# Running sums seeded into PSUM and copied back by ScalarE, and the conditioning as sums of products along the free axis on VectorE

## The chip, the cores and the metric

The kernel runs on one core of a Trainium2 chip. The metric is device time of one execution in microseconds (us). Engines are named as in the profile: PE is TensorE (matrix products; PEld its weight loads), DVE is VectorE, ACT is ScalarE, POOL is GpSimd, SP is SyncE, whose in-order queue issues nearly all DMAs of this kernel. Every engine works through its own queue in order and waits there for the others by semaphores.

## The reference

One layer of a decoder block on 256 tokens of width 4096, in float32:

```
mod = silu(c) @ w_ada + b_ada                      # c: one row of 4096; w_ada 4096 x 12288
shift, scale, gate = split(mod, 3)
h = rmsnorm(x, norm_g) * (1 + scale) + shift       # 256 x 4096
a_b, a_c, a_x, a_z, b_v, b_g, b_z = split(h @ w_in)  # w_in 4096 x 14336, seven parts of 2048
y_a = a_b * conv3(a_c * a_x) * silu(a_z)           # causal, depthwise
y_b = silu(layernorm(conv31(b_v * sigmoid(b_g)))) * silu(b_z)
x = x + gate * (concat(y_a, y_b) @ w_out)          # w_out 4096 x 4096
out = rmsnorm(x, final_g)
```

## The kernel before

**Products.** Each operand of the two projections is split in two 12-bit parts, and three of the four cross products are summed: hi*hi, hi*lo, lo*hi. A *step* loads 512 KB of weights (2 contraction tiles of 128 by 512 columns) into a tile of the pool `raws`; ScalarE writes the high part (`w_h`, L143), VectorE the low part (`w_l`, L144, raw minus high), and TensorE makes 12 products of 128x128 by 128x512 (2 contraction tiles, 2 token tiles, 3 products, L156 to L158). The pool `split` holds three steps' parts. There are 448 steps of the input projection and 128 of the output projection.

**Order of the products.** The 28 column tiles of the input projection are not finished one after the other: the 32 contraction tiles are cut into six blocks (`BLOCKS`), and in each block every column tile gets its products with that block's contraction tiles. A column tile in one block is a *segment* (`SEGS`). Its products build up in a PSUM tile `ps` (pool `pmm`, three buffers). After the first block ScalarE copies `ps` to SBUF as `acc` (L467); after each later block VectorE adds `ps` to `acc` (L469, 135 times in all). So the conditioning of a block's contraction tiles can be worked out while the products of earlier blocks run.

**Conditioning.** `silu(c) @ w_ada` is a product of one row with 201 MB of weights, loaded as 384 tiles of 512 KB: 256 for shift and scale (`mod`), 128 for the gate. For shift and scale, VectorE multiplies a tile by `silu(c)`, one value a partition, and adds it to `modacc` (L174); then TensorE sums over the partitions with one-column products with ones (`modps`, L197). Of the gate's four groups of 1024 columns, two are made on TensorE (`gateps`, L231, one-column weights, four side by side), two on VectorE (L174); each is summed over the partitions and spread to all of them by a product with a matrix of ones (`gatesum`, L248) and copied out by ScalarE (L240, L249).

**Background work.** `queue` holds closures with the step at which each is due; `next_w` first loads and splits the weights one step ahead (`AHEAD`), then runs what is due. The conditioning of contraction tile k is spread so that it is done before its first use; the gate is spread over four stretches of the last block and the output projection (`GATE_RUN`); the convolution of mixer B (30 taps for each of four groups: four ScalarE multiplications L370, one VectorE addition L371) runs from the last block into the output projection; the epilogue of mixer A and the layernorm of mixer B have their stretches too. Emitted in that order, the work of each engine stands in its queue in about that order.

**Start.** SyncE loads x.T and the conditioning of the first two contraction tiles; row statistics of x come from squares on ScalarE, additions on VectorE and products with ones on TensorE (L290). Then the first h (`make_h`) and the first products.

Of the kernel before, what the change touches and what calls it, by code (L numbers as in the profile page):

```python
# [37 lines left out]
GATE_PE = (0, 1)    # gate columns (1024 each) worked out on TensorE, the others on VectorE  # L38
GATE_RUN = {0: (0, 70), 1: (70, 115), 2: (115, 185), 3: (185, 231)}  # when, in steps from the last block on
# [16 lines left out]
PK = O_LNB + NB  # L56
# [23 lines left out]
UNITS = [[0, KD]]   # contraction tiles conditioned together: the first, their number  # L80
for _k in range(KD, KT, KD):
    if UNITS[1:] and UNITS[-1][1] == KD and FIRST_USE[_k] - FIRST_USE[_k - KD] < 4:
        UNITS[-1][1] += KD
    else:
        UNITS.append([_k, KD])


# [545 lines left out]
```

## Time and profile before

| | |
|---|---|
| time, three runs | 1729.15, 1729.73, 1729.89 us; median 1729.73 |
| profiled execution: span | 1728.9 us, 0.8 below that median |
| PE / DVE / ACT busy | 97% / 87% / 54% of the span |
| products of a step | 2.72 us with nothing between them |
| DMA | 522 MB, 302 GB/s on average |

The span is the time from the first to the last instruction of one profiled execution. Busy is the time in which an engine has at least one instruction at work. An instruction's shown duration overlaps its successor's on DVE, ACT and PE, so what it costs in a full queue is the distance from its start to the next start. PEld counts the weight loads of TensorE; line L156 has four in each step, so its count divided by four is a count of steps. In the names, `ps`, `pa` and `pb` are the PSUM tiles of the input projection and of the two halves of the output projection.

### The profile page before, as it was taken

Reading aid. Unit: us, or ns where it says so; the run is one execution under the profiler, and the core shown is the slowest. Engines: PE = TensorE matmul, PEld = TensorE weight load, DVE = VectorE, ACT = ScalarE, POOL = GpSimd, SP = SyncE. Lnnn points to the kernel's source line nnn. Section 1 sums busy time; section 2 is a strip of 40 time slices with the busy share of each in tenths; the row PEclk is TensorE's granted clock in tenths of the full one; section 3 lists DMA queues with packets and bytes.
Section 4 is the critical chain, followed back from the end, with each engine's and each line's share of the span. In section 5 each row is a group of like instructions: output and inputs, shape, how many; then the busy total and the mean of one; then the engine's idle time right before and its main releaser. Section 6 shows DMA issues by size and latency. Waiting matters only on the chain.

```text
span 1728.9 us, 21319 instructions
## 1 busy us (share of the span) xinstructions
PE 1669.5 (97%) x7480; PEld 1340.1 (78%) x7480; DVE 1506.9 (87%) x1490; ACT 937.0 (54%) x1304; POOL 2.9 (0%) x10
## 2 busy tenths in 40 slices
PE   2899999999999999999999999999999999999997
PEld 1778788888888888888888877777777887878885
DVE  7887998899898988898898857898998999989996
ACT  3555443443334333343333468888887888564443
POOL 0000000000000000000000000000000000000000
PEclk8899999999999999999999999999999999999998
DMA  9899899999999998999899977766888888779993
GB/s 387 327 317 331 300 344 327 325 320 332 310 335 326 330 326 302 312 352 329 292 340 321 327 243 248 253 230 232 288 278 281 277 286 280 266 254 335 361 345 116
DMA packets 145715, 522.42 MB, mean 302 GB/s; under 512 B 16196, under 2 KB 16196, under 8 KB 145608
## 3 DMA queue, kind: packets, MB, share of 16 engines
q1 hardware_dynamic: 145464, 520.71, 85.8%
q8 instruction: 58, 0.95, 0.2%
q10 hardware_dynamic: 144, 0.35, 0.1%
q14 instruction: 49, 0.40, 0.1%
HBM read 516.81 MB, written 4.19 MB: 301 GB/s over the span
## 4 chain that ended last, share of the span: by engine, by line
PE 86%; DVE 6%; DMA 4%; issue 3%; ACT 1%; SPq 0%; DVEq 0%; ACTq 0%
PE ps L156 23%; PE ps L157 23%; PE ps L158 23%; PE pb L158 3%; PE pb L156 3%; PE pb L157 3%; DVE w_l L144 2%; PE gateps L231 2%; DMA gate<-in_w_gate 2%; DVE cv L371 1%; PE pa L157 1%; PE pa L158 1%; DVE modacc L174 1%; PE pa L156 1%; DMA mod<-in_w_mod 1%
## 5 line engine op out<-in xcount | busy, mean ns | idle before, releaser
L143 ACT CAST w_h<-w_r 128x1024 fp32r<-128x1024 f32 x576 | 603.7, 1052 | 654.2 <-PE ps L158 490.4
L144 DVE TENSOR_TENSOR w_l<-w_r,w_h 128x1024 fp32r<-128x1024 f32 x576 | 700.8, 1220 | 118.8 <-ACT w_h L143 113.2
L156 PE MATMUL ps<-w_h,hT 128*128 128x512 f32 x1792 | 705.8, 394 | 3.0 <-ACT hT L162 2.6
L157 PE MATMUL ps<-w_l,hT 128*128 128x512 f32 x1792 | 700.7, 391 | 5.6 <-DVE w_l L144 5.6
L158 PE MATMUL ps<-w_h,hT 128*128 128x512 f32 x1792 | 699.4, 390 | 0.0
L156 PEld LDWEIGHTS ps<-w_h,hT 128*128 128x128 f32 x1792 | 337.5, 188 | 96.8 <-issue 10.8
L157 PEld LDWEIGHTS ps<-w_l,hT 128*128 128x128 f32 x1792 | 337.5, 188 | 79.9 <-DVE w_l L144 10.9
L158 PEld LDWEIGHTS ps<-w_h,hT 128*128 128x128 f32 x1792 | 337.3, 188 | 70.6
L174 DVE SCALAR_TENSOR_TENSOR modacc<-mod,cact,modacc 128x512 f32<-128x512 f32 (+1 forms) x341 | 337.4, 990 | 4.6 <-DMA mod<-in_w_mod 1.5
L370 ACT ACTIVATE pr<-uT,pks 128x255 f32<-128x255 f32 (+14 forms) x480 | 198.1, 487 | 2.1 <-DVE cv L371 1.6
L469 DVE TENSOR_TENSOR acc<-ps,acc 128x1024 f32<-128x1024 f32 x135 | 164.9, 1221 | 22.9 <-PE ps L158 22.4
L371 DVE TENSOR_TENSOR cv<-cv,pr 128x1020 f32<-128x1020 f32 (+14 forms) x120 | 138.7, 1156 | 27.1 <-ACT pr L370 26.4
L157 PE MATMUL pa<-w_l,yT 128*128 128x512 f32 x256 | 100.6, 393 | 2.4 <-DVE w_l L144 2.4
L156 PE MATMUL pa<-w_h,yT 128*128 128x512 f32 x256 | 100.1, 391 | 0.0
L156 PE MATMUL pb<-w_h,yT 128*128 128x512 f32 x256 | 100.1, 391 | 0.0
L158 PE MATMUL pb<-w_h,yT 128*128 128x512 f32 x256 | 100.0, 391 | 0.0
L158 PE MATMUL pa<-w_h,yT 128*128 128x512 f32 x256 | 100.0, 390 | 0.0
L157 PE MATMUL pb<-w_l,yT 128*128 128x512 f32 x256 | 99.6, 389 | 0.0
L174 DVE SCALAR_TENSOR_TENSOR gateacc<-gate,cact,gateacc 128x1024 f32<-128x1024 f32 x62 | 79.4, 1280 | 5.8 <-DMA gate<-in_w_gate 5.6
L157 PEld LDWEIGHTS pa<-w_l,yT 128*128 128x128 f32 x256 | 48.0, 188 | 14.6 <-DVE w_l L144 4.8
L467 ACT COPY acc<-ps 128x1024 f32<-128x1024 f32 x28 | 28.5, 1017 | 51.7 <-PE ps L158 51.7
L156 PEld LDWEIGHTS pb<-w_h,yT 128*128 128x128 f32 x256 | 48.1, 188 | 10.3 <-ACT w_h L143 0.2
(129 smaller groups left out, 645.2 us busy)
## 6 DMA issues: line engine op xcount, KB each, us to landing
w_r<-in_w_in SPq DMA_DIRECT2D x448, 512.0 KB, 5.2
mod<-in_w_mod SPq DMA_DIRECT2D x256, 512.0 KB, 5.1
gate<-in_w_gate SPq DMA_DIRECT2D x128, 512.0 KB, 4.8
w_r<-in_w_out SPq DMA_DIRECT2D x128, 512.0 KB, 5.1
xs<-in_xt SPq DMA_DIRECT2D x8, 512.0 KB, 10.2
xr<-in_x SPq DMA_DIRECT2D x8, 512.0 KB, 7.0
out<-o SPq DMA_DIRECT2D x16, 256.0 KB, 2.7
xc<-in_xt SPq DMA_DIRECT2D x4, 512.0 KB, 5.2
```

What stands on the lines that cost most here:

```text
L143: nc.scalar.copy(hi, raw)
L144: nc.vector.tensor_tensor(out=lo, in0=raw, in1=hi.bitcast(F32), op=ALU.subtract)
L156: nc.tensor.matmul(out, ah, hi[:, i], start=f, stop=False)
L157: nc.tensor.matmul(out, ah, lo[:, i], start=False, stop=False)
L158: nc.tensor.matmul(out, al, hi[:, i], start=False, stop=l)
L174: nc.vector.scalar_tensor_tensor(out=acc, in0=raw, scalar=cact[:, j:j + 1], in1=acc, op0=ALU.mult, op1=ALU.add)
L231: nc.tensor.matmul(state["ps"][r:r + 1, 0], cact[:, j + i:j + i + 1], raws_[i][:, h * CT:(h + 1) * CT], start=j == 0, stop=j == KT - 2)
L370: nc.scalar.activation(out=pr[:, j, sh:], in_=u[:, j, :S - sh], func=AF.Copy, scale=cbw[:, 4 * i + j, TAPS - 1 - sh:TAPS - sh])
L371: nc.vector.tensor_tensor(out=o[:, :, sh:], in0=o[:, :, sh:], in1=pr[:, :, sh:], op=ALU.add)
L467: nc.scalar.copy(acc[e], ps)
L469: nc.vector.tensor_tensor(out=acc[e], in0=ps, in1=acc[e], op=ALU.add)
```

## The change

Two things are rewritten, with what follows from them.

1. *Running sums.* `acc` is no longer added on VectorE. Before a segment with earlier sums, ScalarE copies `acc` into the PSUM tile (`seed`), the products add to it, and ScalarE copies the tile back (`take`, with Silu for the z tiles of mixer B). `take` is emitted in the next segment's first step, the seed of the next segment in the last step of the present one.
2. *Conditioning.* The weights are laid out transposed: the 128 outputs of a tile are the partitions, 1024 of the 4096 inputs lie along the free axis. `silu(c)` is spread once to all partitions (`cB`: four row loads, products with ones, Silu). A tile takes one VectorE instruction that multiplies it with its part of `cB` and sums along the free axis, started from the bias or the sum before; four of them make 128 outputs. No sum over partitions is left. The gate's 128 tiles are all done like this, spread over steps 0 to 170 from the last block on; the finished gate is transposed, written to device memory and loaded back spread over the partitions, in four loads beside those of `final_g`.
3. `raws` has 7 tiles instead of 10 (the room goes to `cB`); the row statistics of x are emitted ahead of the conditioning of the first two contraction tiles and summed over all of x on VectorE before TensorE; the first weights are loaded before the last four conditioning tiles. The comments are gone, so that line numbers differ.

```diff
-    raws = ctx.enter_context(tc.tile_pool(name="raws", bufs=10))
+    raws = ctx.enter_context(tc.tile_pool(name="raws", bufs=7))
...
+    def broadcast_c():
+        for q in range(D // ROW):
+            row = bigt(f"crow{q}", (P, ROW))
+            nc.sync.dma_start(row[:1], c[:, q * ROW:(q + 1) * ROW])
+            ps = pmm.tile([P, NS, CT], F32, tag="ps", name=f"cps{q}")
+            for h in range(2):
+                nc.tensor.matmul(ps[:, h], ones[:1], row[:1, h * CT:(h + 1) * CT], start=True, stop=True)
+            nc.scalar.activation(out=cB[:, q * ROW:(q + 1) * ROW], in_=ps, func=AF.Silu)
+
+    def ada_steps(name, srcs, bias, dst):
...
+        def step(q):
+            raw = rawt(f"{name}_{q}", (P, ROW))
+            nc.sync.dma_start(raw, srcs[q])
...
+            nc.vector.tensor_tensor_reduce(out=raw, in0=raw, in1=cB[:, q * ROW:(q + 1) * ROW], scale=1.0, scalar=p[:, q - 1:q] if q else bias, op0=ALU.mult, op1=ALU.add, accum_out=dst if q == D // ROW - 1 else p[:, q:q + 1])
...
+    def gate_finish():
+        ps = misc("gate_ps", (P, P))
+        nc.tensor.transpose(ps[:KT], gateT, ident)
+        row = rawt("gate_row", (P, P))
+        nc.scalar.copy(row[:KT], ps[:KT])
+        nc.sync.dma_start(gate_d.rearrange("(k p) -> k p", p=P), row[:KT])
...
-    for ci, (t0, t1) in GATE_RUN.items():
-        spread(gate_steps(ci), start_last + t0, start_last + t1)
+    spread(gate_steps(), start_last + GATE_RUN[0], start_last + GATE_RUN[1])
...
+    def seed(n):
+        _, e, k0, _ = SEGS[n]
         ps = pmm.tile([P, NS, CT], F32, tag="ps", name=f"ps{k0}_{e}")
-        for k in range(k0, k1, KD):
-            parts = next_w()
-            step += 1
-            products(ps, hT, parts, k, k == k0, k + KD == k1)
-        if k0 == 0:
+        if k0:
+            nc.scalar.copy(ps, acc[e])
+        return ps
+
+    def take(e, k1, ps):
+        if e not in acc:
             acc[e] = bigt(f"acc{e}")
-            nc.scalar.copy(acc[e], ps)
-        else:
-            nc.vector.tensor_tensor(out=acc[e], in0=ps, in1=acc[e], op=ALU.add)
+        nc.scalar.activation(out=acc[e], in_=ps, func=AF.Silu if k1 == KT and e >= 24 else AF.Copy)
...
+    ps = seed(0)
+    for n, (b, e, k0, k1) in enumerate(SEGS):
+        for k in range(k0, k1, KD):
+            parts = next_w()
+            step += 1
+            while pending:
+                pending.pop()()
+            if k + KD == k1 and n + 1 < len(SEGS):
+                ps_next = seed(n + 1)
+            products(ps, hT, parts, k, k == 0, k + KD == k1, seeded=k0 > 0)
+        pending.append(lambda e=e, k1=k1, ps=ps: take(e, k1, ps))
+        ps = ps_next
```

How the queues change is shown at three places. The first is VectorE's queue in the last block, from the split of step 401's weights on, before (`cv` with `pr`: a convolution tap; `yfA`: the epilogue of mixer A):

```order
L144 TENSOR_TENSOR w401_l_9319<-w401_r_9316,w401_h_9318 128x1024
L371 TENSOR_TENSOR cv1_7999<-cv1_7999,pr1_16_9322 128x4x240
L469 TENSOR_TENSOR acc13_606<-ps24_13_9209,acc13_606 128x1024
L144 TENSOR_TENSOR w402_l_9346<-w402_r_9343,w402_h_9345 128x1024
L371 TENSOR_TENSOR cv1_7999<-cv1_7999,pr1_17_9349 128x4x239
L326 TENSOR_TENSOR acc1_653<-acc1_653,acc13_606 128x1024
L144 TENSOR_TENSOR w403_l_9380<-w403_r_9377,w403_h_9379 128x1024
L340 SCALAR_TENSOR_TENSOR yfA1_0_9355<-psA4_9356,pks_88,yfA1_0_9355 128x255
L340 SCALAR_TENSOR_TENSOR yfA1_0_9355<-psA4_9356,pks_88,yfA1_0_9355 128x254
L341 TENSOR_TENSOR yfA1_0_9355<-yfA1_0_9355,psA4_9356 128x256
L371 TENSOR_TENSOR cv1_7999<-cv1_7999,pr1_18_9383 128x4x238
```

and in the changed kernel, where L138 is the weight split, L348 the tap, L317 the epilogue of mixer A, and L186 is the new sum of products (`gate12` is the gate of outputs 1536 to 1663) with the short read of its accumulator behind it:

```order
L138 TENSOR_TENSOR w401_l_9374<-w401_r_9371,w401_h_9373 128x1024
L348 TENSOR_TENSOR cv1_8035<-cv1_8035,pr1_16_9377 128x4x240
L138 TENSOR_TENSOR w402_l_9399<-w402_r_9396,w402_h_9398 128x1024
L186 ISA gate12_3_9402,gateT_94<-gate12_3_9402,cB_95,partgate12_9301 128x1024
L186 ISA gateT_94 128x1
L348 TENSOR_TENSOR cv1_8035<-cv1_8035,pr1_17_9405 128x4x239
L301 TENSOR_TENSOR acc5_730<-acc5_730,acc9_685 128x1024
L303 TENSOR_TENSOR acc1_642<-acc1_642,acc13_597 128x1024
L138 TENSOR_TENSOR w403_l_9429<-w403_r_9426,w403_h_9428 128x1024
L186 ISA gate13_0_9432,partgate13_9434<-gate13_0_9432,cB_95,pks_90 128x1024
L186 ISA partgate13_9434 128x1
L317 SCALAR_TENSOR_TENSOR yfA1_0_9436<-psA4_9437,pks_90,yfA1_0_9436 128x255
```

The addition L469 is gone, and two sums and two reads stand between the same weight splits. The second place is ScalarE's queue there, before:

```order
L143 CAST w402_h_9345<-w402_r_9343 128x1024
L370 ACTIVATE pr1_17_9349<-uT1_7986,pks_88 128x239
L325 ACTIVATE acc13_606<-acc13_606 128x1024
L143 CAST w403_h_9379<-w403_r_9377 128x1024
L338 ACTIVATE yfA1_0_9355<-psA4_9356,pks_88 128x256
L370 ACTIVATE pr1_18_9383<-uT1_7986,pks_88 128x238 x4
L338 ACTIVATE yfA1_0_9355<-psA5_9389,pks_88 128x256
L143 CAST w404_h_9415<-w404_r_9413 128x1024
```

and now (L137 the high part of the weights, L347 the taps, L435 a seed, L443 a take, L302 a Silu of mixer A):

```order
L137 CAST w401_h_9373<-w401_r_9371 128x1024
L347 ACTIVATE pr1_17_9405<-uT1_8022,pks_90 128x239 x4
L435 COPY ps24_10_9485<-acc10_524 128x1024
L443 ACTIVATE acc13_597<-ps24_13_9254 128x1024
L137 CAST w402_h_9398<-w402_r_9396 128x1024
L302 ACTIVATE acc13_597<-acc13_597 128x1024
L137 CAST w403_h_9428<-w403_r_9426 128x1024
L435 COPY ps24_2_9610<-acc2_499 128x1024
L137 CAST w404_h_9460<-w404_r_9458 128x1024
L137 CAST w405_h_9501<-w405_r_9499 128x1024
```

Two seeds and a take have come between the weight parts. The third place is SyncE's queue in the output projection, in the changed kernel (L132 loads weights, L182 gate weights):

```order
L182 DMA gate31_3_12123<-in_w_gate 128x1024
L132 DMA w503_r_12138<-in_w_out 128x1024
L132 DMA w504_r_12166<-in_w_out 128x1024
L210 DMA gate_d_96<-gate_row_12151 32x128
L132 DMA w505_r_12205<-in_w_out 128x1024
L132 DMA w506_r_12223<-in_w_out 128x1024
L132 DMA w507_r_12246<-in_w_out 128x1024
L132 DMA w508_r_12282<-in_w_out 128x1024
```

The write of the finished gate, `gate_d`, which waits for a ScalarE copy, now stands ahead of the load of step 505's weights.

## Rows read from the trace of the kernel before

**Rows 1.** The page's parts 1 and 2: busy times; granted clock in tenths.

```profile
PE 1669.5 (97%) x7480; PEld 1340.1 (78%) x7480; DVE 1506.9 (87%) x1490; ACT 937.0 (54%) x1304; POOL 2.9 (0%) x10
...
PEclk8899999999999999999999999999999999999998
```

**Rows 2.** Windows by stage: us, busy of PE, PEld, DVE, ACT, POOL, clock, DMA, GB/s.

```profile
0.00:50.80 50.80, 12.75 (x41) 9.81 (x41) 38.45 (x56) 18.00 (x20) 0.99 (x8) 0.79 0.98 388
50.80:241.90 191.10, 185.06 (x793) 148.86 (x794) 166.12 (x192) 95.90 (x100) 0.00 (x0) 0.98 0.90 318
241.90:993.90 752.00, 752.00 (x3369) 623.24 (x3368) 668.68 (x621) 303.85 (x303) 0.00 (x0) 1.00 0.92 325
993.90:1538.40 544.50, 541.78 (x2506) 412.63 (x2506) 473.87 (x464) 434.59 (x772) 1.91 (x2) 1.00 0.77 259
1538.40:1728.90 190.50, 177.90 (x779) 145.57 (x777) 159.73 (x160) 84.66 (x110) 0.00 (x0) 0.97 0.81 297
1353.80:1538.40 184.60, 181.88 (x809) 148.22 (x808) 176.23 (x166) 142.83 (x240) 0.00 (x0) 1.00 0.79 264
```

**Rows 3.** Windows of line L156 alone: PE and PEld (four loads a step).

```profile
241.90:993.90 752.00, 424.04 (x1088) 204.06 (x1088) 1.00 0.92 325
993.90:1538.40 544.50, 280.03 (x704) 132.15 (x705) 1.00 0.77 259
551.20:638.20 87.00, 49.76 (x128) 24.02 (x128) 1.00 0.92 326
```

**Rows 4.** The chain in order of time: start, duration, what (x instructions).

```profile
46.29 1.88 PE modps L197 x8
...
337.24 1.68 PE modps L197 x16
...
1192.59 1.72 PE gatesum L248 x4
```

**Rows 5.** Lines 993.9 to 1538.4: shapes, count, busy, mean ns, idle before.

```profile
L144 DVE TENSOR_TENSOR w_l<-w_r,w_h 128x1024 fp32r<-128x1024 f32 x176 | 213.5, 1220 | 26.2 <-ACT w_h L143 25.4
...
L143 ACT CAST w_h<-w_r 128x1024 fp32r<-128x1024 f32 x175 | 182.3, 1046 | 85.7 <-PE ps L158 45.5 <-PE pa L158 30.8 <-issue 5.2
...
L174 DVE SCALAR_TENSOR_TENSOR gateacc<-gate,cact,gateacc 128x1024 f32<-128x1024 f32 x31 | 39.7, 1281 | 5.7 <-DMA gate<-in_w_gate 5.6
...
L231 PE MATMUL gateps<-gate,cact 128*1 128x512 f32 x248 | 35.3, 591 | 0.0
...
L469 DVE TENSOR_TENSOR acc<-ps,acc 128x1024 f32<-128x1024 f32 x28 | 34.2, 1221 | 6.3 <-PE ps L158 6.2
```

**Rows 6.** Timeline of DVE: start, duration, instruction.

```profile
398.09 1.22 DVE L144 TENSOR_TENSOR w_l<-w_r,w_h 128x1024 fp32r<-128x1024 f32 x1
399.22 1.28 DVE L174 SCALAR_TENSOR_TENSOR modacc<-mod,cact,modacc 128x1024 f32<-128x1024 f32 x1
400.42 1.22 DVE L144 TENSOR_TENSOR w_l<-w_r,w_h 128x1024 fp32r<-128x1024 f32 x1
```

**Rows 7.** Timeline of ACT: a sum of squares' accumulator read (L524).

```profile
1569.29 0.19 ACT L524 ACTIVATION_READ_ACCUMULATOR xr<-o 128x1 f32 x1
1569.38 0.62 ACT L524 ACTIVATE xr<-o 128x512 f32<-128x512 f32 x1
```

**Rows 8.** DMA issues: count, size, median us to landing.

```profile
w_r<-in_w_in SPq DMA_DIRECT2D x448, 512.0 KB, 5.2
```

**Rows 9.** The page's part 5: the copy out of PSUM.

```profile
L467 ACT COPY acc<-ps 128x1024 f32<-128x1024 f32 x28 | 28.5, 1017 | 51.7 <-PE ps L158 51.7
```

**Rows 10.** Window of line L174 alone, 241.9 to 993.9: DVE.

```profile
241.90:993.90 752.00, 236.73 (x211) 1.00 0.92 325
```

**Rows 11.** Waits of SyncE's queue: us in total, times, longest.

```profile
SPq L138 <- DVE w_l L144: 513.8, 310, 7.0
```

**Rows 12.** Windows of two stretches with waits, columns as in Rows 2.

```profile
80.00:100.00 20.00, 17.14 (x70) 13.04 (x69) 16.20 (x22) 10.64 (x14) 0.00 (x0) 0.91 0.96 341
1424.00:1432.00 8.00, 7.04 (x32) 5.46 (x31) 7.14 (x7) 6.82 (x15) 0.00 (x0) 1.00 0.81 269
```

More of the change, by code (lines that the diff above doesn't have):

```diff
@@ L37 @@
 HOLD = 5
[L38 to L39 removed]
+ROW = 1024
+GATE_RUN = (0, 170)
 A_SPAN = 5
@@ L55 @@
 O_LNB = O_LNG + NB
-PK = O_LNB + NB
+O_BGATE = O_LNB + NB
+PK = O_BGATE + KT
 def _segments():
@@ L79, with decoder_block @@
     FIRST_USE.setdefault(_k, _t)
[L80 to L83, printed above, removed]
-    else:
-        UNITS.append([_k, KD])
 @with_exitstack
-def decoder_block(ctx: ExitStack, tc: tile.TileContext, x, c, w_mod, w_gate, w_in, w_out, xt, pk, b_gate, final_g, out):
+def decoder_block(ctx: ExitStack, tc: tile.TileContext, x, c, w_mod, w_gate, w_in, w_out, xt, pk, final_g, out):
     nc = tc.nc
@@ L145, in load_w, with products @@
         return hi, lo
-    def products(ps, act, parts, k0, first, last, tokens=range(NS)):
+    def products(ps, act, parts, k0, first, last, tokens=range(NS), seeded=False):
         hi, lo = parts
@@ new lines, in broadcast_c @@
+    def broadcast_c():
[7 more added lines that the diff above has]
+    def ada_steps(name, srcs, bias, dst):
+        state = {}
+        def step(q):
+            raw = rawt(f"{name}_{q}", (P, ROW))
+            nc.sync.dma_start(raw, srcs[q])
+            if q == 0:
+                state["part"] = part.tile([P, 4], F32, tag="part", name=f"part{name}")
+            p = state["part"]
+            nc.vector.tensor_tensor_reduce(out=raw, in0=raw, in1=cB[:, q * ROW:(q + 1) * ROW], scale=1.0, scalar=p[:, q - 1:q] if q else bias, op0=ALU.mult, op1=ALU.add, accum_out=dst if q == D // ROW - 1 else p[:, q:q + 1])
+        return [lambda q=q: step(q) for q in range(D // ROW)]
@@ new lines, in mod_steps @@
+    def mod_steps(k):
+        def finish():
+            nc.vector.scalar_tensor_tensor(out=gscT[:, k:k + 1], in0=modT[:, 32 + k:33 + k], scalar=1.0, in1=pks[:, O_G + k:O_G + k + 1], op0=ALU.add, op1=ALU.mult)
+        work = []
+        for t in (1, 0):
+            col = 32 * t + k
+            work += ada_steps(f"mod{k}_{t}", w_mod[k, t], pks[:, O_BADA + col:O_BADA + col + 1], modT[:, col:col + 1])
+        return work + [finish]
+    gate_d = dram.tile([D], F32, name="gate_d")
+    gate = {}
@@ new lines, in gate_finish, with gate_steps @@
+    def gate_finish():
[4 more added lines that the diff above has]
+        nc.sync.dma_start(gate_d.rearrange("(k p) -> k p", p=P), row[:KT])
+    def gate_steps():
+        work = [f for k in range(KT) for f in ada_steps(f"gate{k}", w_gate[k], pks[:, O_BGATE + k:O_BGATE + k + 1], gateT[:, k:k + 1])]
+        return work + [gate_finish]
+    plan = [(w_in[e], k) for _, e, k0, k1 in SEGS for k in range(k0, k1, KD)]
@@ new lines, in decoder_block, with load_ahead @@
+    end_in = len(plan)
+    start_last = sum((k1 - k0) // KD for b, _, k0, k1 in SEGS if b < len(BLOCKS) - 1)
+    conv_end = end_in + CONV_END
+    plan += [(w_out[dt], k0 + k) for k0 in (0, KT // 2) for dt in range(NDT) for k in range(0, KT // 2, KD)]
+    loaded = []
+    step = 0
+    def load_ahead(last):
+        while len(loaded) <= min(last, len(plan) - 1):
+            src, k = plan[len(loaded)]
+            loaded.append(load_w(src, k, f"w{len(loaded)}", 0 <= len(loaded) - len(plan) + KT // 2 // KD < HOLD))
@@ L284, in x_stats @@
             nc.scalar.activation(out=sq, in_=xc, func=AF.Square)
-            if ci % 2 == 0:
+            if ci == 0:
                 total = sq
-                continue
-            nc.vector.tensor_tensor(out=total, in0=total, in1=sq, op=ALU.add)
-            for i in range(4):
-                nc.tensor.matmul(ps, ones, total[:, i], start=ci + i == 1, stop=ci + i == 10)
+            else:
+                nc.vector.tensor_tensor(out=total, in0=total, in1=sq, op=ALU.add)
+        for i in range(4):
+            nc.tensor.matmul(ps, ones, total[:, i], start=i == 0, stop=i == 3)
         y = const.tile([P, S], F32, name="x_rstd")
@@ L294, in x_stats @@
         return y
-    first_steps = mod_steps(0, KD)
-    for f in first_steps[:2]:
-        f()
-    rstd = x_stats()
-    for f in first_steps[2:]:
+    broadcast_c()
+    rstd = x_stats()
+    first_steps = [f for k in range(KD) for f in mod_steps(k)]
+    for f in first_steps[:-4]:
+        f()
+    load_ahead(AHEAD)
+    for f in first_steps[-4:]:
         f()
@@ L441, in decoder_block @@
     hull = [(0, KD)]
-    need = [(max(FIRST_USE[k] - LEAD, 1), k + n) for k, n in UNITS[1:]]
+    need = [(max(FIRST_USE[k] - LEAD, 1), k + KD) for k in range(KD, KT, KD)]
     while hull[-1][1] < KT:
@@ L479, in decoder_block @@
             zB[e - 24] = acc[e]
-            nc.scalar.activation(out=acc[e], in_=acc[e], func=AF.Silu)
         elif 12 <= e < 16:
```

123 lines of the change are left out of this document (26 added, 97 removed).

## The prediction

> **What bounds the kernel now.** I read the page's first two parts, then busy time by stage, then the groups of one stage, then single stretches. The page says TensorE 97% busy, VectorE 87%, ScalarE 54% [rows 1]. Such an average hides which stage has which limit, so I cut the span at step boundaries (L156's weights are loaded four times a step) into five stages: S0 to 50.8 us (no products yet), S1 to 241.9 (64 steps), S2 to 993.9 (272 steps), S3 to 1538.4 (176 steps: the last block of the input projection and the first half of the output projection), S4 the rest [rows 2, 3].
>
> A step costs TensorE 87.0 / 32 = 2.72 us where little else is in its stream [rows 3]. S2 takes 752.0 us against 272 x 2.72 = 739.8: 12 us over, about what the conditioning's sums on ones take, pieces of 1.68 us [rows 4]. S3 takes 544.5 against 176 x 2.72 = 478.7: 66 us over, of which 35.3 are the gate's one-column products L231 and 3.4 two pieces of sums on ones for the gate [rows 4, 5]; the rest stays as it is. TensorE is busy 541.8 of the 544.5 us: S3 is TensorE's too, but VectorE has 473.9 us of busy time beside it and ScalarE 434.6 [rows 2]. That stage decides this change.
>
> **The change part by part.** TensorE loses the gate's products and all sums on ones, and gets eight small products at the start and one transpose. In S3 its need falls to 544.5 - 35.3 - 3.4 = 506 us.
>
> VectorE loses in S3 the 28 additions L469 (34.2 us) and 31 gate multiply-adds with the multiplication that begins them (39.7 + 0.7) [rows 5]. It gets 127 of the gate's 128 new sums of products: the gate, before on two engines and spread over S3 and S4, is wholly VectorE's and ends within S3. Its order shows it: two sums in three steps where none stood.
>
> The price of a sum is not in the trace. From below: a two-source 128x1024 instruction shows 1.22 us and starts its successor after 1.13 (398.09 to 399.22) [rows 6]; no row with two f32 sources of that size is faster. Nearest is the multiply-add L174, also two f32 sources and one scalar a partition: 1.20 to the next start (399.22 to 400.42) [rows 6]. A sum also reads out its accumulator in an instruction of its own; the only such read shown is ScalarE's, which holds the queue 1569.38 - 1569.29 = 0.09 us [rows 7]. From above: product and sum as two passes, 1.13 + 1.20 + 0.09 = 2.42. I take 1.20 + 0.09 = 1.29, by the nearest rows; the range keeps 1.13 and 2.42.
>
> So VectorE's need in S3 becomes 473.9 - 34.2 - 40.4 + 127 x 1.29 = 563 us, over TensorE's 506 and over the 544.5 that the stage takes now. The low parts of the weights stand in the same queue behind these sums, and the split pool holds three steps, so VectorE cannot work ahead by more: TensorE will wait for w_l. The bound moves from TensorE to VectorE. How full does a queue with such handovers get? In the last 64 steps of S3 VectorE is busy 176.2 of 184.6 us, 95%, with TensorE nearly full too [rows 2]; 563 / 0.95 would be 590. I take 578, between the two, and count into it what SyncE's queue adds: the gate's write waits for a ScalarE copy with step 505's weights queued behind it; a load lands 5.2 us after its issue [rows 8], some 7.4 with both parts of the split, against 4 to 5 us of products ready on chip, so about 3 us once. S3: +33.5 us.
>
> ScalarE gets in S3 28 copies out of and 26 into PSUM, about 1.02 us each by L467 [rows 9]; a copy into PSUM is not in the trace, and a fifth more or less on these is 5 us of its time. It loses the gate's twelve copies of 512 columns, 7 us at somewhat over half of L467's time. 434.6 + 54 x 1.02 - 7 = 483 of 578 us: not the bound, but 84% of an in-order queue that also makes the high part of the weights, which is why I don't take 563. In S2 it gets 187 copies beside 303.9 of 752 us [rows 2]. VectorE there loses 236.7 us of multiply-adds [rows 10] and 94 additions (1.22 us each, 115) and gets 186 x 1.29 = 240: 557 of 752. S1 and S2 stay TensorE's.
>
> Gains outside S3: in S2 the sums on ones, 11 of the 12 us. In S1, 17 us over 64 x 2.72, they and smoother conditioning give 5; the first products at half clock and the rate of the loads stay. In S4 two gate pieces of 1.72, so 3; the four added gate loads are hidden, issued a column tile ahead. In S0 a piece of 1.88 us before the first product goes [rows 4], but the broadcast of c (four loads, eight products, four Silu) now stands before the first sum: 1.
>
> Sum on the profiled execution: 1728.9 + 33.5 - 11 - 5 - 3 - 1 = 1742.4; the median of the runs is 0.8 above its span: **1743 us**, 0.8% slower.
>
> The load ring falls from 10 to 7 tiles. SyncE waits for its tiles all through the run (513.8 us on w_l alone [rows 11]), so it is always full. In S2 272 + 186 tiles pass in 272 steps, 1.68 a step, so 7 last 11.3 us, and a load needs 5.2 [rows 8]. I cost this at nothing; the 6 us left are its cover.
>
> [...] The multiply-add L174, with two f32 sources in SBUF, takes 1281 ns against 1220 for the plain L144 [rows 5]. [...]
>
> **Rivals.**
> A, faster: a sum costs the plain 1.13, its read is hidden, handovers cost nothing. VectorE's need in S3 is then 399.3 + 127 x 1.13 = 543, the stage stays at 544.5, and the gains of 20 us, perhaps 25, remain: 1705 to 1710. For it: neighbours on VectorE overlap by 0.08 [rows 6], and the last 64 steps of S3 kept VectorE 95% busy, so handovers can cost little. Against: a read that needs its sum's result leaves less to overlap. It decides from a price under about 1.2 on.
> [...]
> C, much slower: two passes. 127 x (2.42 - 1.29) = 144 in S3; in S2 VectorE needs 557 + 186 x 1.13 = 767, 25 more than TensorE; 16 sums stand before the first product, 18: about 1930.
> D, slower: the shorter ring. If its cover fails and each step of S2 loses 0.1 us, 27: 1770.
>
> **How the numbers follow.** Forecast 0.48, own range 1725 to 1762 (a price of 1.20 to 1.35, S3 at 560 to 597); A 0.24, B 0.13, C 0.07, D 0.08. The three runs lie within 0.7 us; 0.2%, 3.5 us, is about what a measurement can tell from no change. Faster: A and 0.04 of the forecast's low end, 0.28. Same: the forecast from 1726 to 1733, 0.12. Slower: the rest, 0.60. The range, 1704 to 1784, leaves out C, A's low tail and the top of B and D.
>
> **What would show it.** In the profile after: S3 near 578 us, VectorE over 95% busy in it and TensorE waiting for w_l in most of its steps; 384 sums of about 1.28 us, each with a short read; S2 at 740 to 742 us; no granted clock below 1.00 in S3. I am wrong if S3 takes 544 us or less, which makes the price or the fill of the queue the mis-sized term, or if S1 or S2 lengthen, by loads or by ScalarE's copies ahead of the weight split.

## The result, and the profile after

The changed kernel takes 1769.70 us (median of four runs, 1769.41 to 1770.85), the kernel before beside it 1729.81: ratio 1.0232, 95% interval 1.0217 to 1.0246. Forecast: 1743. The direction was right; of 40 us lost, 13 were forecast.

Windows by stage of the changed kernel, cut at the same steps, columns as in [rows 2]; the last line is the last 64 steps of S3:

```profile
0.00:52.90 52.90, 17.77 (x24) 7.66 (x24) 36.48 (x53) 21.30 (x23) 0.99 (x8) 0.88 0.87 321
52.90:240.10 187.20, 183.61 (x769) 144.83 (x769) 147.62 (x189) 121.75 (x129) 0.00 (x0) 0.99 0.92 329
240.10:1001.10 761.00, 759.85 (x3265) 614.38 (x3264) 563.55 (x685) 466.46 (x490) 0.00 (x0) 1.00 0.91 318
1001.10:1578.00 576.90, 535.65 (x2249) 417.20 (x2248) 553.17 (x659) 471.74 (x812) 0.00 (x0) 0.97 0.83 280
1578.00:1769.10 191.10, 178.47 (x771) 144.57 (x769) 122.18 (x126) 81.84 (x106) 0.00 (x0) 0.98 0.65 221
1378.50:1578.00 199.50, 191.61 (x809) 149.38 (x808) 191.60 (x221) 140.23 (x233) 0.00 (x0) 0.98 0.83 285
```

S3 is where the forecast put it: 576.9 us, VectorE 96% busy. S2 is not: 761.0 us instead of 741, though TensorE lost all sums on ones and waits for almost nothing (busy 759.85). It is busy longer with fewer instructions (3265 instead of 3369), so each must take longer. The window of the first product's line (L150) over 32 steps, answering the last of [rows 3], says so:

```profile
552.90:642.10 89.20, 50.46 (x129) 24.11 (x128) 1.00 0.91 318
```

89.2 / 32 = 2.788 us a step instead of 2.72, at the same clock of 1.00. TensorE's weight loads, by starts, first in the kernel before, then in the changed one (one step is 12 of them):

```profile
599.90 0.19 PEld L156 LDWEIGHTS ps<-w_h,hT 128*128 128x128 f32 x1
600.13 0.19 PEld L157 LDWEIGHTS ps<-w_l,hT 128*128 128x128 f32 x1
...
602.62 0.19 PEld L156 LDWEIGHTS ps<-w_h,hT 128*128 128x128 f32 x1
```

```profile
600.04 0.19 PEld L150 LDWEIGHTS ps<-w_h,hT 128*128 128x128 f32 x1
600.27 0.19 PEld L151 LDWEIGHTS ps<-w_l,hT 128*128 128x128 f32 x1
...
602.83 0.19 PEld L150 LDWEIGHTS ps<-w_h,hT 128*128 128x128 f32 x1
```

A load takes 0.19 us in both, but 2.79 instead of 2.72 us pass from the first to the thirteenth. Nothing waits; the products themselves are 2.5% slower, in S1, S2 and S4 alike (from a load to the twelfth after it, median of the stage: 2.72 us before in each of the three, 2.79 now).

The page's part 5, costliest groups of the changed kernel, answering [rows 5, 9]:

```profile
L443 ACT ACTIVATE acc<-ps 128x1024 f32<-128x1024 f32 x163 | 167.1, 1025 | 234.2 <-PE ps L152 233.9
L435 ACT COPY ps<-acc 128x1024 f32<-128x1024 f32 x135 | 137.2, 1017 | 0.4
L186 DVE CUSTOM_DVE_ANT_0 gate<-gate,cB,partgate 128x1024 f32<-128x1024 f32 x96 | 122.8, 1279 | 0.4
```

and VectorE's timeline round one gate sum, answering [rows 6, 7]:

```profile
1525.78 1.27 DVE L186 CUSTOM_DVE_ANT_0 gate<-gate,cB,pks 128x1024 f32<-128x1024 f32 x1
1526.98 0.07 DVE L186 DVE_READ_ACCUMULATOR2_ANT partgate<- 128x1 f32 x1
1526.98 1.21 DVE L138 TENSOR_TENSOR w_l<-w_r,w_h 128x1024 fp32r<-128x1024 f32 x1
```

A sum costs its successor 1526.98 - 1525.78 = 1.20 us, as much as a multiply-add [rows 6]; the read of the accumulator starts together with the next instruction and costs nothing here. A copy into PSUM takes as long as one out of it (1017 and 1025 ns). What TensorE waits for most in S3 (PEld: before a weight load, PE: before a product; us in all, times, longest):

```profile
PEld ps L151 <- DVE w_l L138: 33.1, 29, 3.0
PE ps L151 <- DVE w_l L138: 21.9, 22, 2.5
PEld pa L151 <- DVE w_l L138: 14.1, 21, 2.3
```

It is the low parts, as forecast, but not in most steps: 29 + 21 = 50 weight loads wait for them in 176 steps, 47.2 us together. The granted clock, 1.00 in S3 before, is 0.97: seven stretches of 3.4 to 6.8 us, 31 us in all, have a granted clock of 0.50, with products 0.43 us apart instead of 0.23 (1170.16 to 1170.58; 1173.32 to 1173.55). Each begins within 1.3 us of the end of a wait of TensorE of 0.9 to 3.3 us. Not every such wait was followed by one: after 2.4 us at 1240.2 the clock stayed at 1.00.

### The profile page after: what moved, and what is told of

Read it like the earlier page. It is cut to its first block, busy times and chain, and to the rows that moved or that the text cites. A ratio compares the mean times of both kernels' runs of the same rounds, so it can differ in the third digit from the quotient of the medians.

```text
span 1769.1 us, 20848 instructions
## 1 busy us (share of the span) xinstructions
PE 1675.3 (95%) x7073; PEld 1328.7 (75%) x7073; DVE 1423.0 (80%) x1707; ACT 1163.1 (66%) x1558; POOL 1.0 (0%) x8
## 4 chain that ended last, share of the span: by engine, by line
PE 66%; DVE 17%; issue 9%; ACT 4%; DMA 4%; DVEq 0%; ACTq 0%
PE ps L151 18%; PE ps L152 17%; PE ps L150 17%; DVE w_l L138 5%; DVE cv L348 5%; DVE gate L186 3%; PE pb L152 3%; PE pb L150 3%; PE pb L151 3%; DMA mod<-in_w_mod 2%; ACT w_h L137 2%; DMA gate<-in_w_gate 1%; ACT pr L347 1%; DVE mod L186 1%; PE pa L151 1%
## 5 line engine op out<-in xcount | busy, mean ns | idle before, releaser
L138 DVE TENSOR_TENSOR w_l<-w_r,w_h 128x1024 fp32r<-128x1024 f32 x576 | 700.5, 1222 | 257.6 <-ACT w_h L137 252.0
L137 ACT CAST w_h<-w_r 128x1024 fp32r<-128x1024 f32 x576 | 598.9, 1045 | 279.0 <-PE ps L152 148.4
L151 PE MATMUL ps<-w_l,hT 128*128 128x512 f32 x1792 | 717.0, 400 | 26.4 <-DVE w_l L138 26.4
L150 PE MATMUL ps<-w_h,hT 128*128 128x512 f32 x1792 | 711.8, 398 | 25.9 <-ACT hT L156 17.8
L152 PE MATMUL ps<-w_h,hT 128*128 128x512 f32 x1792 | 712.3, 398 | 0.8 <-DVE hT L157 0.8
L150 PEld LDWEIGHTS ps<-w_h,hT 128*128 128x128 f32 x1792 | 340.4, 190 | 109.9 <-ACT hT L156 18.9
L443 ACT ACTIVATE acc<-ps 128x1024 f32<-128x1024 f32 x163 | 167.1, 1025 | 234.2 <-PE ps L152 233.9
L186 DVE CUSTOM_DVE_ANT_0 mod<-mod,cB,partmod 128x1024 f32<-128x1024 f32 x192 | 245.6, 1279 | 28.0 <-DMA mod<-in_w_mod 26.3
L347 ACT ACTIVATE pr<-uT,pks 128x255 f32<-128x255 f32 (+14 forms) x480 | 196.9, 487 | 1.1 <-DVE cv L348 1.1
L348 DVE TENSOR_TENSOR cv<-cv,pr 128x1020 f32<-128x1020 f32 (+14 forms) x120 | 138.7, 1156 | 4.5 <-ACT pr L347 4.3
L435 ACT COPY ps<-acc 128x1024 f32<-128x1024 f32 x135 | 137.2, 1017 | 0.4
L186 DVE CUSTOM_DVE_ANT_0 gate<-gate,cB,partgate 128x1024 f32<-128x1024 f32 x96 | 122.8, 1279 | 0.4
L151 PE MATMUL pa<-w_l,yT 128*128 128x512 f32 x256 | 104.6, 409 | 6.3 <-DVE w_l L138 6.1
L150 PE MATMUL pa<-w_h,yT 128*128 128x512 f32 x256 | 101.6, 399 | 1.6 <-ACT w_h L137 1.6
L150 PE MATMUL pb<-w_h,yT 128*128 128x512 f32 x256 | 101.0, 394 | 0.0
L186 DVE CUSTOM_DVE_ANT_0 mod<-mod,cB,pks 128x1024 f32<-128x1024 f32 x64 | 81.9, 1279 | 12.4 <-DMA mod<-in_w_mod 12.4
```

The source lines that it names most:

```text
L137: nc.scalar.copy(hi, raw)
L138: nc.vector.tensor_tensor(out=lo, in0=raw, in1=hi.bitcast(F32), op=ALU.subtract)
L150: nc.tensor.matmul(out, ah, hi[:, i], start=f, stop=False, skip_group_check=seeded)
L151: nc.tensor.matmul(out, ah, lo[:, i], start=False, stop=False, skip_group_check=seeded)
L152: nc.tensor.matmul(out, al, hi[:, i], start=False, stop=l, skip_group_check=seeded)
L186: nc.vector.tensor_tensor_reduce(out=raw, in0=raw, in1=cB[:, q * ROW:(q + 1) * ROW], scale=1.0, scalar=p[:, q - 1:q] if q else bias, op0=A ...
```

## The experiments

Stage times come from one profile each, cut at steps 0, 64, 336 and 512; the last column is the median of the runs. A profiled run can lie off that median: that of "parts first" is 4.5 us under it, that of "gate in four" 3.8 over, so a few us between two stages are not resolved.

| kernel | S0 | S1 | S2 | S3 | S4 | us |
|---|---|---|---|---|---|---|
| before | 50.8 | 191.1 | 752.0 | 544.5 | 190.5 | 1729.8 |
| changed | 52.9 | 187.2 | 761.0 | 576.9 | 191.1 | 1769.7 |
| parts first | 52.9 | 183.9 | 741.7 | 571.7 | 187.0 | 1743.4 |
| gate in four | 53.9 | 184.4 | 744.2 | 546.8 | 202.9 | 1730.2 |
| running sums alone | 51.7 | 186.3 | 752.2 | 561.4 | 190.5 | 1742.2 |
| conditioning alone | 53.9 | 186.0 | 746.3 | 597.2 | 187.0 | 1773.5 |
| sums, not in the last block | 50.9 | 188.4 | 752.1 | 547.8 | 190.5 | 1731.9 |
| mix | 54.8 | 184.1 | 744.0 | 551.4 | 199.1 | 1735.4 |
| gate early | 53.8 | 184.7 | 770.6 | 551.0 | 187.1 | 1746.7 |
| gate in free steps | 53.0 | 185.0 | 774.3 | 550.3 | 187.1 | 1751.9 |
| shift and scale alone | 54.5 | 185.1 | 757.9 | 551.5 | 196.6 | 1746.9 |

**Why are the products slower?** In the kernel before, the pool `big` (with h, the stationary operand) and the pool `split` (the weight parts, the moving operand) start 44 tiles of 4096 bytes apart in each partition: 33 tiles of `big`, 1 of `ada`, 10 of `raws`. In the changed kernel it is 44 again (33, the four of `cB`, 7 of `raws`), but the four small tiles of partial sums (pool `part`) lie between them too: 128 bytes more. Theory P: that distance sets the pace. Theory C: something else in the changed kernel does. The pool is moved ahead of `big`:

```diff
+    part = ctx.enter_context(tc.tile_pool(name="part", bufs=4))
     big = ctx.enter_context(tc.tile_pool(name="big", bufs=33))
     cbc = ctx.enter_context(tc.tile_pool(name="cbc", bufs=1))
-    part = ctx.enter_context(tc.tile_pool(name="part", bufs=4))
```

> The changed kernel with one edit: the pool of the four 16-byte partial sums (128 bytes in all) is laid out ahead of the big pool instead of behind cB, so that the tiles of the stationary operand (big: h and y) and of the moving operand (split: weight parts) lie again a whole number of 4096 bytes apart in every partition, as in the kernel before; in the changed kernel they are 128 bytes off that. Theory P (the two operands' places in SBUF set the pace of the products: 2.72 us a step before, 2.79 after, in every stage): steps of S2 back to 2.72 us, S2 about 742 us instead of 761, S4 about 187, the whole 1769.7 - 19 - 4 - 4 and a little in S3 = 1738 to 1745. Theory C (the slower products come from the new work beside them, seeds and takes in PSUM or the sums on VectorE): no change, 1769 to 1771, steps of 2.79.

1743.36 us (1738.86 to 1745.52), ratio to before 1.0081, interval 1.0064 to 1.0098. S2 is back at 741.7 / 272 = 2.73 us a step, S1 and S4 are 3.3 and 4.1 us shorter than in the changed kernel: 26.3 us of the loss came from where a pool stands in a list. The opposite is an unused tile in the kernel before, between `big` and `raws` (128, 64 or 256 bytes), ahead of everything, or between `raws` and `split`:

```diff
     big = ctx.enter_context(tc.tile_pool(name="big", bufs=33))
+    padp = ctx.enter_context(tc.tile_pool(name="padp", bufs=1))
+    padt = padp.tile([P, 32], F32, name="padt")
+    nc.gpsimd.memset(padt, 0.0)
```

> The kernel before with one edit: an unused tile of 128 bytes a partition between the big pool and the load ring, so that the weight parts lie 128 bytes off a whole number of 4096 from h and y. Nothing of the work changes. Theory P: steps of 2.79 us in S2 and everywhere that TensorE bounds, 576 x 0.069 = 40 us, about 1768. Theory C: 1730, steps of 2.72.

> The kernel before with the unused 128 bytes ahead of everything, so that all big tiles and all weight parts move together. If only the distance of the two operands counts: 1730, steps of 2.72. If the absolute place of the weight parts counts: as the run with the gap, about 1768.

> The kernel before with a gap of 64 bytes instead of 128. Theory P has no size for it: any distance that is not a whole number of 4096 slows alike (about 1768), or the loss goes with the distance (between 1730 and 1768). Theory C: 1730.

> The kernel before with an unused tile of 128 bytes between the pools raws and split: h and the raw weights keep their distance, the split weights move 128 bytes from both. Theory P1 (it is the distance of TensorE's own two operands, h and the split weights, that sets the products' pace): 2.79 us a step and 1760 to 1765, as with the gap ahead of raws. Rival P2 (it is the distance of h from the raw tiles, which DMA writes and ScalarE reads): 2.72 us and 1730.

> The kernel before with 256 unused bytes between big and raws. 64 bytes gave products 0.2289 us apart, 128 bytes 0.2323, none 0.2267. Theory P3 (only the distance within some period counts, and 256 or 512 bytes are such a period, since h's and the weights' blocks already lie at many multiples of 512): 0.2267 us or a little off it, 1728 to 1745. Rival P4 (the pace falls with the distance as far as it goes): 0.235 us or more, above 1775.

128 bytes: 1762.76 us, ratio 1.0189 (1.0174 to 1.0205), with nothing of the work changed. The others are single runs. All shifted by 128: 1729.38. 64 bytes: 1743.38. 128 bytes between the raw weights and `split`: 1764.56, so it is the distance of TensorE's two operands that counts, and not that to the raw tiles. 256 bytes: 1729.78, no loss. The window of the first product's line with 128 bytes, and the whole window of the kernel with 256 (32 steps in each):

```profile
552.90:642.10 89.20, 50.46 (x129) 24.12 (x128) 1.00 0.92 319
```

```profile
552.90:639.94 87.04, 87.04 (x385) 72.07 (x384) 77.64 (x66) 33.79 (x33) 0.00 (x0) 1.00 0.93 327
```

89.20 and 87.04 us: 2.79 and 2.72 a step. P holds. Since 256 bytes cost nothing, and the blocks of h and of the weights that meet in a product lie at many multiples of 512 bytes from each other before any gap is added, the remainder of the distance by 256 fits every run. That rests on one run at 256, and why the place counts was not tried.

**Is S3 VectorE's?** With the pace restored, take the gate out of S3 in part; or give VectorE its additions back; or take away the wait in SyncE's queue that the forecast priced at 3 us.

```diff
-GATE_RUN = (0, 170)
+GATE_RUN = {0: (0, 65), 1: (65, 130), 2: (130, 195), 3: (180, 226)}
```

> Changed kernel with the four small partial-sum tiles ahead of the big ones (so the operands' distance in SBUF is again that of the kernel before), and the gate's 128 sums not in steps 0 to 170 of the last block on, but in four groups of 32 over steps 0 to 65, 65 to 130, 130 to 195 and 180 to 226, each transposed by itself and written to device memory on ScalarE's queue. Theory V (in the last block and the first half of the output projection VectorE's need is the bound, at 1.20 us a sum): about 40 sums leave that stage, its need falls from 552 to some 504 us, TensorE's is 506, so the stage falls from 571.7 us to 530 to 540 and the time to 1700 to 1712. Rival W (the stage is long because TensorE waits once a step for handovers, or because its clock falls after each gap, whatever VectorE's load): it stays above 560 and the time at 1735 or more.

```diff
-        if k0:
-            nc.scalar.copy(ps, acc[e])
...
+            nc.vector.tensor_tensor(out=acc[e], in0=ps, in1=acc[e], op=ALU.add)
```

> Changed kernel with the four partial-sum tiles first (operands' distance as before) and without the running sums' rewrite: VectorE adds ps to acc as in the kernel before. So it is the conditioning alone, at the old pace of products. Theory V: in the last block and half of the output projection VectorE's need rises by the 28 additions, 34 us, to about 586 us; at the fill of 96% seen there the stage takes 605 to 612, and the time is 1773 to 1785. Rival W (handovers and clock, not VectorE's load): about 1743, as with the running sums rewritten.

```diff
-        nc.sync.dma_start(gate_d.rearrange("(k p) -> k p", p=P), row[:KT])
+        nc.scalar.dma_start(gate_d.rearrange("(k p) -> k p", p=P), row[:KT])
```

> Changed kernel with the four partial-sum tiles first, and the finished gate written to device memory by a DMA issued from ScalarE's queue and not SyncE's, so that no weight load stands behind it. Theory Q (the write's wait in SyncE's queue leaves TensorE without weights around step 505): steps 496 to 512, 3.7 us each, fall to about 3.2 and the time by 3 to 8 us, to 1735 to 1740. Rival: those steps are long because of the layernorm's work there, and the time stays within 2 us of 1743.

S3 with the parts first, with the gate in four, and with VectorE's additions back (columns as in [rows 2]):

```profile
978.40:1550.10 571.70, 527.73 (x2249) 412.75 (x2249) 552.59 (x659) 471.54 (x813) 0.00 (x0) 0.98 0.84 283
982.50:1529.30 546.80, 515.84 (x2251) 413.79 (x2250) 506.98 (x583) 469.33 (x812) 0.00 (x0) 0.98 0.79 258
986.20:1583.40 597.20, 535.26 (x2250) 411.38 (x2248) 584.22 (x688) 431.11 (x765) 0.00 (x0) 0.98 0.81 271
```

The stage follows VectorE's load both ways, though less than us for us. With the additions back VectorE is busy 31.6 us more and S3 takes 25.5 more, at 98% busy: 1773.49 us (1.0248, 1.0233 to 1.0263), the low end of theory V. With the gate in four VectorE is busy 45.6 us less and S3 takes 24.9 less; that is between V's 530 to 540 us and W's 560, nearer to V, and with VectorE and TensorE both near 510 us the stage still takes 547. But S4 grows by 16, so that the time is in neither theory's range and the kernel ties with the one before: 1730.15 us, 0.9996 (0.9987 to 1.0005). ScalarE's waits for VectorE in S4 (in all, times, longest), in the kernel before and with the gate in four:

```profile
ACT xr L524 <- DVE o L519: 6.7, 4, 4.7
```

```profile
ACT xr L513 <- DVE o L508: 27.4, 7, 6.6
```

The squares wait for the residual's addition, which stands among gate sums in VectorE's queue, and the next weights' high part stands behind the squares.

The write on ScalarE's queue changes nothing: 1744.07 us. ScalarE's timeline of this kernel in the output projection shows the wait that I had put on SyncE:

```profile
1510.84 1.06 ACT L137 CAST w_h<-w_r 128x1024 fp32r<-128x1024 f32 x1 [0.70 <-PE pa L152]
1520.56 0.26 ACT L209 COPY gate_row<-gate_ps 32x128 f32<-32x128 f32 x1 [8.66 <-PE gate_ps L207]
...
1522.83 2.92 ACT L137 CAST w_h<-w_r 128x1024 fp32r<-128x1024 f32 x3
```

ScalarE stands 8.66 us before its copy of the transposed gate, which TensorE reaches late in its own queue (in the changed kernel at 1544.0, 5.4 us after the last gate sum), and three steps' high parts stand behind it. Two steps take 7.9 and 7.1 us instead of 2.72: 9.6 us, once. Not all of it is this wait's: TensorE waits 4.5 us in them (0.77, 1.95 and 1.73), and the rest is products of the layernorm and products at a lower granted clock (0.51 from 1524 to 1531). The changed kernel has the same wait, 8.6 us, and a granted clock of 0.50 from 1548.5 to 1555.3.

**What do the running sums cost?**

> The kernel before with the running sums alone changed: ScalarE copies them into PSUM and back, the conditioning stays as it was, and so does the operands' distance in SBUF. Theory V: VectorE was not the bound before, so taking 135 additions (165 us) from it wins nothing, and ScalarE has the room: 1725 to 1733, no change. Rival S (ScalarE's copies stand ahead of the weights' high parts in its in-order queue, and TensorE waits for them): 1740 to 1760.

> The run with the running sums alone (1742.2 us), but in the last block VectorE adds ps to acc as in the kernel before; the earlier blocks keep ScalarE's copies. Theory S (in the last block ScalarE's 54 copies stand ahead of the weights' high parts and of the convolution's multiplications, and cost the 17 us by which that stage grew, 544.5 to 561.4): the stage returns to 543 to 548 us and the time to 1722 to 1728. Rival (the copies in the earlier blocks move the work so that the last stage comes out worse): 1738 or more.

The first is the kernel before with part 1 of the change and nothing else; the second differs from it by

```diff
+    def seeded(n):
+        return SEGS[n][2] > 0 and SEGS[n][0] < len(BLOCKS) - 1
...
-        nc.scalar.activation(out=acc[e], in_=ps, func=AF.Silu if k1 == KT and e >= 24 else AF.Copy)
+        if k1 == KT:
+            nc.vector.tensor_tensor(out=acc[e], in0=ps, in1=acc[e], op=ALU.add)
+        else:
+            nc.scalar.copy(acc[e], ps)
```

1742.17 us (1.0061, 1.0044 to 1.0078) and 1731.89 (1.0008, 0.9998 to 1.0017). So ScalarE's copies in the last block cost some 10 us here, with VectorE less busy than before (446.6 us instead of 473.9) and ScalarE at 476 of 561. S3 of the first:

```profile
990.20:1551.60 561.40, 552.80 (x2507) 413.97 (x2506) 446.62 (x436) 475.98 (x822) 1.91 (x2) 1.00 0.74 252
```

and VectorE's two longest waits in it:

```profile
DVE cv L371 <- ACT pr L370: 46.5, 69, 4.1
DVE w_l L144 <- ACT w_h L143: 40.8, 43, 2.7
```

Before, these were 26.4 and 25.4 us: taps and high parts, both made by ScalarE, come later behind its copies. The 34 us that VectorE saves in additions it spends waiting.

**Can the parts be put together better?** The mix has the gate's groups 0 and 1 on TensorE as before, 2 and 3 as sums, and the additions of the run above; "gate early" puts 32 of the 128 sums ahead of the last block. The first edit is against the changed kernel, the second against the gate in four.

```diff
-GATE_RUN = (0, 170)
+GATE_PE = (0, 1)
+GATE_RUN = {0: (0, 70), 1: (70, 115), 2: (115, 176), 3: (176, 224)}
```

> Changed kernel with the four partial-sum tiles first; the conditioning of shift and scale as sums of products; the gate's first two groups on TensorE as in the kernel before, its last two as sums of products with their own transpose and write; running sums by ScalarE's copies up to the last block, by VectorE's additions in it. By the stages measured so far: start 53.9, first 64 steps 184.4, next 272 steps 742 (no sums on ones), last block and half the output projection 545 as before (TensorE's gate products are back, VectorE is at 470), rest 187 to 190: 1712 to 1716. Rival (that stage needs VectorE's work of the kernel before in its order, and new handovers cost 10 to 20 us there): 1722 to 1732.

> As the run with the gate in four, but its first group of 32 sums is spread over 250 steps before the last block, where VectorE is busy 563 of 744 us, and the other three over steps 0 to 174 from the last block on; nothing of the gate is left in the second half of the output projection. Theory G (the 16 us that were lost there, 202.9 instead of 187, came from the gate's last group: its sums and handovers in a stage where VectorE was full): last stage 187 to 189; earlier stages as measured (53.9, 184.4, 744 to 747), last block and half the output projection 540 to 552: 1710 to 1720. Rival R (that stage lost its time to the shorter ring of 7 tiles, and 32 more loads before the last block, 338 GB/s instead of 325, lose 10 to 20 us there in the same way): 1722 to 1735.

```diff
-GATE_RUN = {0: (0, 65), 1: (65, 130), 2: (130, 195), 3: (180, 226)}
+GATE_RUN = {0: (-256, -6), 1: (0, 58), 2: (58, 116), 3: (116, 174)}
```

The mix: 1735.40 us (1.0029, 1.0018 to 1.0040), beyond even the rival's 1732: S3 6 us and S4 10 us over what was expected. Early: 1746.70 (1.0091, 1.0075 to 1.0108). S4 is back at 187, so its loss was the gate's last group, but S2 grew by 26, with VectorE far from full. Two more, made from the mix with one gate group on TensorE, gave the same S2:

```diff
-GATE_PE = (0, 1)
-GATE_RUN = {0: (0, 70), 1: (70, 115), 2: (115, 176), 3: (176, 224)}
+GATE_PE = (1,)
+GATE_RUN = {0: (-256, -6), 1: (0, 60), 2: (60, 118), 3: (118, 176)}
```

> As the mix (1735.4 us), but the gate's first group as sums of products before the last block, only its second on TensorE (17.6 us instead of 35.3), the last two as sums by step 176; running sums added by VectorE in the last block. Theory G: last stage 187 to 189; last block and half the output projection with TensorE at 524 us and VectorE at 399.3 + 34.2 + 64 x 1.20 = 510: 538 to 550; in all 1706 to 1718. Rival R: 1722 to 1735.

> As the run before it in this call, but in the last block too the running sums go by ScalarE's copies, so VectorE's need there is 476 us and TensorE's 524. Theory S (54 ScalarE copies in the last block cost 10 to 17 us of handovers, as in the run with the running sums alone): 6 to 15 us slower than that run. Rival V (the fuller of VectorE and TensorE decides, and VectorE's 34 us less help): 3 to 10 us faster than it, 1700 to 1712.

1755.77 us (1.0147, 1.0132 to 1.0162) with additions in the last block (S2 773.1, S3 555.4) and 1750.06 (1.0112, 1.0097 to 1.0127) with copies (772.9, 549.1). So ScalarE's copies in the last block won 5.7 us here, against theory S, and its copies in all blocks won 30 between the conditioning alone and the parts first (1773.5 and 1743.4); they cost 10 us where the conditioning was the old one. What they are worth seems to go by how full VectorE is. Next, each early sum in a step that has no other:

```diff
+    taken = {int(np.ceil(t)) for t, _ in queue}
+    free = [t for t in range(start_last - 272, start_last - 6) if t not in taken]
+    work = gate_steps(0)
+    for i, f in enumerate(work):
+        queue.append((float(free[i * (len(free) - 1) // (len(work) - 1)]), f))
```

> As the run with the gate's first group of 32 sums before the last block (1746.7 us), but each of the 32 is emitted in a step in which no sum of shift and scale is due (62 of the 269 steps there have none), so no step has two. Theory T (a step loses time when two sums stand ahead of its weights' low part in VectorE's queue; the totals have room, 563 of 744 us): the third stage returns from 770.6 to 744 to 748 us, the others stay (53.8, 184.7, 551, 187): 1720 to 1726. Rival L (the loads: 325 GB/s rises to 343 and the ring of 7 tiles holds less time): it stays above 760 us and the time above 1736.

1751.90 us (1.0121, 1.0104 to 1.0138): theory T falls. The time is on L's side, but L has no support in the trace: in S2 ScalarE waits only 2.3 us for loads of weights, and VectorE for none. What grew is ScalarE's wait before its copies out of PSUM, in S2 of the parts-first kernel and of this one:

```profile
ACT acc L443 <- PE ps L152: 151.5, 93, 1.7
```

```profile
ACT acc L449 <- PE ps L152: 213.2, 93, 5.0
```

What differs is ScalarE's order. Round step 87, in the parts-first kernel and in this one:

```
L137 CAST w87_h_2190<-w87_r_2188 128x1024
L137 CAST w88_h_2210<-w88_r_2208 128x1024
L443 ACTIVATE acc3_392<-ps2_3_2131 128x1024
L435 COPY ps2_25_2322<-acc25_315 128x1024
```

```
L137 CAST w87_h_2200<-w87_r_2198 128x1024
L449 ACTIVATE acc3_392<-ps2_3_2141 128x1024
L441 COPY ps2_25_2335<-acc25_315 128x1024
L137 CAST w88_h_2223<-w88_r_2221 128x1024
```

Both kernels emit step 88's high part ahead of these two copies (`next_w` splits one step ahead), so a queue need not keep the order of emission: with the sum added the copies stand ahead of that part. Timeline of ScalarE there:

```profile
296.64 2.00 ACT L137 CAST w_h<-w_r 128x1024 fp32r<-128x1024 f32 x2
302.78 1.03 ACT L449 ACTIVATE acc<-ps 128x1024 f32<-128x1024 f32 x1 [4.15 <-PE ps L152]
303.84 1.02 ACT L441 COPY ps<-acc 128x1024 f32<-128x1024 f32 x1
304.80 1.04 ACT L137 CAST w_h<-w_r 128x1024 fp32r<-128x1024 f32 x1
```

ScalarE stands 4.15 us before the take, until TensorE ends the old segment, and only then makes the part for the step after the one that TensorE is starting. Steps 87 and 88 take 3.31 and 3.89 us; 1.8 us are gone. This is read from order and trace, and it is not shown: a run with the order held fixed was not made.

Last, shift and scale alone as sums (the gate as before, which takes 4 KB more and leaves a ring of 6 tiles):

```diff
...
-    raws = ctx.enter_context(tc.tile_pool(name="raws", bufs=7))
+    ada = ctx.enter_context(tc.tile_pool(name="ada", bufs=1))
+    raws = ctx.enter_context(tc.tile_pool(name="raws", bufs=6))
...
```

> The kernel before with the conditioning of shift and scale alone as sums of products (with the new start), the gate wholly as before (two groups on TensorE, two as multiply-adds), running sums by ScalarE's copies up to the last block and by VectorE's additions, emitted where they were, in it; operands' distance as before, 6 tiles in the load ring. Theory H (each part's stage cost adds up where the stage's handovers stay as they were): start 54, 184, 742 to 744, then 545 and 190.5 as in the kernel before: 1714 to 1720. Rival R (a ring of 6 tiles is too short, or the last two stages come out worse by 10 us through any other order): 1726 to 1740.

> The same with the running sums added by VectorE in all blocks: the conditioning of shift and scale alone is changed. Theory H: VectorE needs 557 + 115 = 672 of some 742 us in the third stage and stays under TensorE's time; 4 us were lost there when VectorE added (746 against 742): 1716 to 1724. Rival: with VectorE at 90% in the third stage the low parts come late and the sums on ones are paid back: 1728 or more.

1746.89 us (1.0092, 1.0074 to 1.0110) and, with VectorE adding in every block, 1750.50 (1.0112, 1.0099 to 1.0125). VectorE's wait for shift and scale weights in S2, in the mix (7 tiles) and here (6):

```profile
DVE mod L190 <- DMA mod<-in_w_mod: 28.9, 23, 3.6
```

```profile
DVE mod L189 <- DMA mod<-in_w_mod: 58.6, 50, 3.5
```

It doubles, with low parts queued behind it, which speaks for the rival: 6 tiles are too few. No run changed the ring alone. No version beat the kernel before; the gate in four and the sums kept out of the last block tie with it.

## Why the prediction was wrong in size

- **The step that failed: "A step costs TensorE 2.72 us", carried over to the changed kernel.** It was read from the kernel before, where it holds, and "S1 and S2 stay TensorE's" took it along. The change put 128 bytes between the operands of every product, and a step became 2.788. S2 was forecast at 741 us and took 761, the largest part of the 27 us by which the forecast fell short. No term of the sum could hold it; moving one line took 26.3 us away.
- **With the pace restored the sum holds, in part by luck:** parts first took 1743.4 us, forecast 1743. By stage, forecast against measured change: S1 -5 and -7.2, S2 -11 and -10.3, S3 +33.5 and +27.2, S4 -3 and -3.5, S0 -1 and +2.1 (why S0 grew was not tried; c's broadcast now stands ahead of its sums). Those changes add up to 8 us and not 13, since the profiled run was 4.5 us under the median: S1, S2 and S4 were right within 2.2 us, S3 some 6 too large in that run.
- **S3's 578 was right by errors that cancel.** That VectorE would bound it was right (its load moved the stage both ways). The price was 1.20 and not 1.29, so VectorE's need was 399.3 + 127 x 1.20 = 552 (busy: 553.2) and not 563. But the stage lost more beside it: 4.5 to 9.6 us once around the gate's transposition, forecast as 3 and on SyncE's queue, where ScalarE's copy was the instruction that waited, and some 5 us of the slower products (576.9 against 571.7, one profile each).
- **Rival C** is out: a sum of products with two f32 sources takes 1279 ns, 5% over the plain 1222, and its read is hidden (the next instruction starts 1.20 us after the sum's start); no run shows a sum at the 2.42 us of two passes.
- **Rival A** counted on 1.13 and on handovers at nothing; the price was 1.20, and S3 did not stay at 544. **Rival B**, 1768 us by a lower granted clock in S3, came in small: clock 0.97 in S3, not 1.00 as forecast, and 0.98 with the pace restored. What that cost was not separated; 31 us at a granted clock of 0.50, with products 0.43 us apart instead of 0.23, lose at most some 14 (an estimate, if TensorE had worked all through them).
- **The ring at no cost** held in S2 with 7 tiles (741.7 us, 2 over 272 steps at 2.72), and, it seems, not with 6. So it is chance that the 1769.7 us measured lie at rival D's 1770, with S2 20 us over its forecast: the same ring costs nothing in S2 once the pace is restored.
- **The signs named beforehand:** S2 did lengthen, to 761 us, but neither by loads nor by ScalarE's copies, the two reasons that were given for it. The 384 sums, each with a short read, and VectorE at 96% in S3 came as said; TensorE waited for low parts in fewer than a third of the steps and not in most.
- ScalarE "not the bound": true by busy time (471.7 of 576.9), but waits behind it cost time that busy time does not show (running sums alone; as far as the order was read, gate early).

## What to carry to other kernels

Before a stage's pace is carried over, compare where the operands lie in the on-chip memory before and after: here a new small tile between two pools slowed every product by 2.5%, and moving one line got it back. Totals of busy time say which engine must bound a stage, not what it will take: look for each instruction that waits on another engine in an in-order queue, and ask what stands behind it. Where the queues do not keep the order of emission, an instruction added in one place can change the order in others (here a gate sum on VectorE and ScalarE's copies round step 87), so read the new order there too.

## What the runs showed of the hardware

- The relative place of a product's two operands sets its pace: 2.72 us for 12 products at the distance of the kernel before (44 x 4096 bytes from pool to pool) and at 256 bytes more, 2.79 at 128 more, 2.75 at 64 more; the whole kernel 1729.8, 1729.8, 1762.8 and 1743.4 us. The distances of 64 and 256 were run once each.
- The accumulator's read after a VectorE sum (0.07 us) delays nothing: the sum's successor starts 1.20 us after it, as after a multiply-add without such a read.
- A copy of 128x1024 into PSUM on ScalarE takes 1017 ns, as out of it.
